# One more seven-product pair in the second MLP, and norm weights multiplied on VectorE: a hybrid decoder trunk on one core

## The chip, the cores and the metric

The kernel runs on one core of a Trainium2 chip. The metric is the device time of one execution in microseconds (us). The kernel before took 1081.53 us (median of three runs, 1081.48 to 1082.1). One execution was taken with the hardware profiler; that one has its own time, given below beside its span.

## The reference

The reference is a two-layer decoder trunk over 512 tokens of width 1024. Layer 0 is a gated short convolution followed by an MLP; after it a shared key and value side is computed. Layer 1 is a sparse attention followed by a second MLP; a final RMS norm ends it. The change is in the second MLP and in the final norm:

```python
def rms_norm(x, g):
    y = xf * lax.rsqrt(jnp.mean(xf * xf, axis=-1, keepdims=True) + EPS)
    return (y * g.astype(jnp.float32)).astype(x.dtype)

def squared_relu_mlp(h, w1, w2):
    return jnp.square(jax.nn.relu(h @ w1)) @ w2      # 1024 -> 4096 -> 1024
...
    x = x + squared_relu_mlp(rms_norm(x, norm_mlp[layer]), mlp_w1[layer], mlp_w2[layer])
return rms_norm(x, final_norm)
```

Everything is float32 in and out. The kernel writes each float32 factor as the sum of a high and a low float16 part and uses three products: high by high, high by low, low by high.

## The kernel before

**Layout.** Activations are kept turned: channels on the 128 partitions, tokens along the free side. `X` is the residual stream, eight tiles of 128 channels by 512 tokens.

**The MLP in two halves.** The 4096 hidden channels are done in two halves of 2048. In each half `mlp_up` makes eight column pairs `p` (256 hidden channels each) and `mlp_down` adds their part to `X` in four column pairs `p` (256 output channels each). The hidden values go to `rh` and `rl` (high and low parts), in seven combinations per pair, for the products of `mlp_down`.

**Two ways for an up pair.** An ordinary pair (`pair`, lines 410 to 412) takes eight chunks of the input, two column tiles and three products: 48 matmuls of 512 columns. A pair of the table `UP_SEVEN` goes through `seven` (line 687): it treats the product as 2x2 blocks and needs seven block products in place of eight: 84 matmuls of 256 columns. For that, its weights must be loaded as blocks and three VectorE instructions per piece add blocks together (lines 156 and 158). And its result is not ready in a bank at the end: four partial results are copied out of PSUM by ScalarE (`keep`, line 698), and three VectorE additions (lines 713, 716, 720) put them together. `seven` uses three accumulators: A and C, two buffers of bank `a` or of bank `c`, taken in turn from pair to pair, and E in bank `b`. A's first product is kept before A's second product is added to it in the same bank, and so on, so TensorE may not write on until the copy is done. After the products `put_relu` squares (ScalarE, line 666), forms differences (VectorE, lines 162 and 164), and writes `rh` (ScalarE, line 669) and `rl` (VectorE, line 670).

**Weights.** SyncE loads pieces of weights in a fixed order. A piece of blocks has 2048 numbers per partition and is loaded by two transfers of 256 KB into one of three buffers `wst2`; an ordinary piece has 1024 numbers per partition and is loaded by one transfer of 512 KB into one of three buffers `wst`. `convert_piece` turns a piece into `whi` and `wlo`. For blocks: sums on VectorE (lines 156, 158), `whi` on ScalarE (line 219), `wlo` on VectorE (line 220), 1792 numbers per partition, into four buffers. For an ordinary piece: `whi` on ScalarE (line 239) and `wlo` on VectorE (line 240), 1024 numbers. All weights of `mlp_down` are blocks: per column pair four pieces, which the text counts through as down piece 0 to 15. The load into a `wst2` buffer waits until the `wlo` of the piece before in that buffer is done.

**Down.** `mlp_down` makes seven products for eight chunks `c`, 21 matmuls of 256 columns each (line 833). Column pairs 0 and 2 use the banks b, b, a, a, and pairs 1 and 3 the banks d, e, c, c. `combine` (lines 799 to 814) adds the finished products into `X` on VectorE.

**The final norm's lead.** In the last half, `mlp_down` calls `mid_b(p)` in each column pair 1 to 3 (in pairs 1 and 2 behind chunk 5, in pair 3 behind chunk 3). It turns the finished column pair `p - 1` back to tokens by rows: eight transposes on TensorE (line 1555) into the two buffers of bank `a` or of bank `c`, four per buffer. Each buffer then holds two tiles of 128 tokens by 256 channels. For each tile ScalarE sums the squares (`square`, line 1551), copies the tile to `xt` (line 1566), and GpSimd multiplies the copy by the norm's weights (line 1567). The next column pair's products use the same two buffers again.

**The order.** The instructions are put in order by a scheduler when the program is built; each engine runs its own queue in that order, and waits on semaphores that the builder sets where two instructions touch the same buffer or the same PSUM bank.

Of the kernel before, what the change touches and what calls it, by code (L numbers as in the profile page):

```python
# [13 lines left out]
AF = mybir.ActivationFunctionType  # L14
OP = mybir.AluOpType
# [36 lines left out]
def body(ctx, tc, x, rel_bias, norm_mix, norm_mlp, mlp_w1, mlp_w2, a_w_in, a_conv_w, a_w_out,  # L52
# [3 lines left out]
    PE, ACT, DVE, POOL = nc.tensor, nc.scalar, nc.vector, nc.gpsimd  # L56
# [11 lines left out]
    def bank(tag, shape=(128, 512)):  # L68
        n = {"a": 2, "b": 2, "c": 2, "d": 1, "e": 1}[tag]
        return psum.tile(list(shape), F32, name=tag, bufs=n)  # L70
# [18 lines left out]
    def mlp_pieces(layer):  # L89

        for half in range(2):
            for p in range(8):
                (blocks if p in UP_SEVEN[layer][half] else block)(mlp_w1[layer], (8 * half + p) * 256, SW)
            for p in range(4):
# [10 lines left out]
            pieces.append(([v[c + k, :, :, c0:c0 + 256] for k in range(2)], None, scale))  # L105

    BY_SEVEN = ((2, 2), (3, 0), (3, 2))
    UP_SEVEN = (((4, 6), (0, 2, 4, 6)), ((6,), (0, 2, 4, 6)))

    v = a_w_in[0].rearrange("(c p) (s n) -> c p s n", p=128, s=3)  # L110
    for c in range(8):
# [315 lines left out]
    def ftile(name, bufs=2, n=S):  # L427
        return wk[0].tile([128, n], F32, name=name, bufs=bufs)
# [82 lines left out]
    for p in range(4):  # L511
# [57 lines left out]
        for i, dst in enumerate((pc, pu, pb)):  # L569
# [19 lines left out]
            for m in range(2):  # L589
                ch = 2 * p + m  # L590
                if dst is pc:
                    if m == 0:
                        tmps = []
                    t = ftile("cv_t", 2)
# [4 lines left out]
                elif dst is pu:  # L599
                    if m == 0:  # L600
                        convs = []
                    v = ftile("cv_v", 2, S + 2)
# [3 lines left out]
                    o = ftile("cv_o", 2)  # L606
# [38 lines left out]
    def mlp_up(xs, ss, rh, layer, half, rb, sums):  # L645
# [80 lines left out]
        def places():  # L726

            tags = 4 * ((wk[0], "up_s", 4),) + ((work, "ssacc", 1), (work, "sq", 1)) + 2 * ((work, "rb", 3),)
            for i in range(0, 8, 2):
                yield [u.tile([128, 4, 256], F16, name=name, bufs=n) for u, name, n in tags[i:i + 2]]  # L730
# [17 lines left out]
        at, staged_sums = places(), {}  # L748
        by_seven = UP_SEVEN[layer][half]
        early = half == 0 and layer == 0 and by_seven  # L750
# [779 lines left out]
    with pool("hidden_b") as hp:  # L1530
# [15 lines left out]
        def gains(p, n=2):  # L1546
            return fng[p // 2][:, (p % 2) * 256:(p % 2) * 256 + n * 128]

        def square(v, t, k, scale=1.0):
            junk = hp.tile([128, 8, 256], F32, name="ml_z", bufs=2)[:, 0, 0:v.shape[1]]  # L1550
            return ACT.activation(junk, v, AF.Square, scale=scale, accum_out=ssf[:, t, k:k + 1])

        def turn_tokens(ps, t, tiles):
            for m, ch in enumerate(tiles):
                PE.transpose(ps[:, m * 128:(m + 1) * 128], X[:, ch, t * 128:(t + 1) * 128], ident)

        def token_major(p, h, tag):

            ps = bank(tag)
            for i in range(2):  # L1560
                turn_tokens(ps[:, i * 256:(i + 1) * 256], 2 * h + i, (2 * p, 2 * p + 1))
            for i in range(2):
                t = 2 * h + i
                v, o = ps[:, i * 256:(i + 1) * 256], xt[t][:, p * 256:(p + 1) * 256]
                square(v, t, p)
                last = ACT.activation(o, v, AF.Copy)
                POOL.tensor_tensor(o, o, gains(p), op=OP.mult)
            return last

        def mid_b(p):  # L1570
            return [token_major(p - 1, h, "a" if p % 2 else "c") for h in range(2)][1]
# [126 lines left out]
```

## Time and profile before

| what | value |
|---|---|
| median of three runs | 1081.53 us |
| profiled execution: its time, its span | 1083.04 us, 1080.0 us |
| TensorE busy | 1067.5 us, 99% of the span |
| VectorE busy | 958.1 us, 89% |
| ScalarE busy | 621.7 us, 58% |
| GpSimd busy | 75.2 us, 7% |
| mean granted TensorE clock | 0.998 |

The second MLP's last half runs from 916.68 us (its first up pair) to the end. Its up pair 6 starts at 975.27, its ordinary pair 7 at 984.44, its down column pairs 0, 1, 2 and 3 at 994.80, 1013.14, 1032.35 and 1051.57, and the transposes of `mid_b` at 1026.90, 1046.11 and 1060.74.

In a row of a timeline stand the start, the duration, the engine and line, the operation and its tiles; the bracket behind it is the idle time just before and what ended it. In a row of the chain stand a start, a duration, the engine, the bank and line. In a row of the waits stand who waited for whom, the time in total, the number of waits and the longest.

### The profile page before, as it was taken

The numbers are of one execution on the slowest core, as the hardware profiler recorded it, in microseconds if no ns is written. First come the engines' busy times: TensorE is split into PE (matmuls) and PEld (weight loads), VectorE is DVE, ScalarE is ACT, GpSimd is POOL, SyncE is SP. The second block draws the span as 40 slices with busy tenths as digits, with TensorE's granted clock in tenths as the row PEclk, the third lists the DMA queues.
The fourth block names the chain that finished last, engine by engine and source line by source line (L and its number), as shares of the span: only waits on it lengthen the run. The fifth ranks groups of instructions, "written<-read, shape, count | busy, mean of one in ns | idle before, by whom it ended". The sixth has DMA issues, their size and how long they took to land.

```text
span 1080.0 us, 21256 instructions
## 1 busy us (share of the span) xinstructions
PE 1067.5 (99%) x8486; PEld 740.5 (69%) x8486; DVE 958.1 (89%) x1688; ACT 621.7 (58%) x974; POOL 75.2 (7%) x113
## 2 busy tenths in 40 slices
PE   9999999999999999999999999999999999999997
PEld 4446644477887758874867677775446788766896
DVE  5898757999998999999478899996999999999996
ACT  5663246565334674548577887874666433566453
POOL 1000000000000000000110104211000000002022
PEclk9999999999999999999999999999999999999999
DMA  8344124333433334312443442201542333333221
GB/s 260 112 147 134 40 81 154 125 99 109 137 101 115 104 113 155 119 44 95 126 139 102 143 138 81 61 21 60 166 127 70 106 111 124 98 101 98 98 99 78
DMA packets 117698, 118.50 MB, mean 110 GB/s; under 512 B 7276, under 2 KB 114496, under 8 KB 117600
## 3 DMA queue, kind: packets, MB, share of 16 engines
q1 hardware_dynamic: 114384, 110.77, 32.6%
q10 hardware_dynamic: 2512, 4.70, 1.3%
q0 software_dynamic: 704, 1.68, 0.5%
q8 instruction: 66, 1.08, 0.4%
q14 instruction: 32, 0.26, 0.1%
HBM read 110.22 MB, written 2.14 MB: 104 GB/s over the span
## 4 chain that ended last, share of the span: by engine, by line
PE 72%; DVE 18%; ACT 3%; issue 3%; DMA 3%; POOL 1%; SPq 0%; ACTq 0%; DVEq 0%; POOLq 0%
PE b L833 6%; PE c L411 5%; PE c L410 5%; PE c L412 4%; PE a L833 4%; PE c L833 4%; PE a L412 4%; PE a L687 4%; PE a L410 4%; PE a L411 4%; DVE wlo L220 4%; PE e L833 3%; PE b L412 3%; PE b L411 3%; PE c L1340 3%
## 5 line engine op out<-in xcount | busy, mean ns | idle before, releaser
L219 ACT ACTIVATE whi<-wst 128x1792 f16<-128x1792 f32 x92 | 153.9, 1692 | 120.9 <-DVE wst L158 72.1
L220 DVE SCALAR_TENSOR_TENSOR wlo<-wst,whi 128x1792 f16<-128x1792 f32 x92 | 185.5, 2022 | 6.5 <-ACT whi L219 6.4
L833 PEld LDWEIGHTS <-whi 128*128 128x128 f16 x1768 | 173.0, 98 | 20.3
L240 DVE SCALAR_TENSOR_TENSOR wlo<-wst,whi 128x1024 f16<-128x1024 f32 (+4 forms) x118 | 129.2, 1101 | 20.6 <-ACT whi L239 20.3
L239 ACT ACTIVATE whi<-wst 128x1024 f16<-128x1024 f32 (+4 forms) x118 | 111.1, 950 | 61.8 <-PE a L411 21.9
L412 PEld LDWEIGHTS <-wlo 128*128 128x128 f16 x800 | 78.1, 98 | 86.5 <-DVE wlo L240 1.0
L410 PEld LDWEIGHTS <-whi 128*128 128x128 f16 x800 | 78.2, 98 | 78.9 <-ACT whi L239 0.6
L411 PEld LDWEIGHTS <-whi 128*128 128x128 f16 x800 | 78.2, 98 | 78.4
L833 PEld LDWEIGHTS <-wlo 128*128 128x128 f16 x884 | 86.5, 98 | 10.9 <-DVE wlo L220 0.2
L669 ACT ACTIVATE rh<-ml_z 128x1792 f16<-128x1792 f32 x32 | 54.1, 1693 | 58.2 <-DVE ml_z L164 58.2
L411 PE MATMUL c<-xsl,whi 128*128 128x512 f16 x224 | 85.0, 379 | 0.0
L412 PE MATMUL c<-xsh,wlo 128*128 128x512 f16 x224 | 85.0, 379 | 0.0
L410 PE MATMUL c<-xsh,whi 128*128 128x512 f16 x224 | 85.0, 379 | 0.0
L1327 ACT ACTIVATE at_p<-at_s,at_m 128x384 f32<-128x384 f32 (+3 forms) x128 | 71.0, 556 | 20.9 <-DVE at_m L1325 20.7
L158 DVE TENSOR_TENSOR wst<-wst 128x256 f32<-128x256 f32 x184 | 78.3, 432 | 2.1
L156 DVE TENSOR_TENSOR wst<-wst 128x512 f32<-128x512 f32 x92 | 63.8, 697 | 15.3 <-DMA wst<-mlp_w_dram 15.1
L833 PE MATMUL b<-rh,whi 128*128 128x256 f16 x256 | 69.2, 273 | 0.0
L833 PE MATMUL b<-rh,wlo 128*128 128x256 f16 x256 | 69.2, 273 | 0.0
L833 PE MATMUL b<-rl,whi 128*128 128x256 f16 x256 | 67.8, 273 | 0.0
L687 PEld LDWEIGHTS <-whi 128*128 128x128 f16 x616 | 60.2, 98 | 7.9
L670 DVE TENSOR_TENSOR rl<-ml_z,rh 128x1792 f16<-128x1792 f32 x32 | 64.7, 2023 | 0.4 <-ACT rh L669 0.4
L1325 DVE CUSTOM_DVE_ANT_0 at_s<-b,T 128x384 f32<-128x384 f32 (+3 forms) x128 | 59.1, 485 | 4.9 <-PE b L1318 4.7
(437 smaller groups left out, 2911.7 us busy)
## 6 DMA issues: line engine op xcount, KB each, us to landing
wst<-mlp_w_dram SPq DMA_DIRECT2D x172, 256.0 KB, 2.9
wst<-mlp_w_dram SPq DMA_DIRECT2D x42, 512.0 KB, 3.7
wst<-a_w_in_dram SPq DMA_DIRECT2D x12, 512.0 KB, 3.5
wst<-w_kv_dram SPq DMA_DIRECT2D x12, 512.0 KB, 3.5
wst<-a_w_out_dram SPq DMA_DIRECT2D x8, 512.0 KB, 3.4
wst<-b_w_qg_dram SPq DMA_DIRECT2D x8, 512.0 KB, 3.6
wst<-b_w_o_dram SPq DMA_DIRECT2D x8, 512.0 KB, 3.6
T<-ext_d ACTq DMA_DIRECT2D x6, 528.0 KB, 3.9
```

The source lines that it names most:

```text
L158: DVE.tensor_tensor(b[:, :, o], b[:, :, x], b[:, :, y], op=OP.add)
L219: ACT.activation(hi, b[:, :, 1:], AF.Copy, scale=sc)
L220: lows[0] = DVE.scalar_tensor_tensor(lo, b[:, :, 1:], sc, hi, op0=OP.mult, op1=OP.subtract)
L239: ACT.activation(hi[:, s:e], w, AF.Copy, scale=sc)
L240: DVE.scalar_tensor_tensor(lo[:, s:e], w, sc, hi[:, s:e], op0=OP.mult, op1=OP.subtract)
L410: PE.matmul(ps, w[0], xs[0], start=start, stop=False, **k)
L411: PE.matmul(ps, w[0], xs[1], start=False, stop=False, **k)
L412: return PE.matmul(ps, w[1], xs[0], start=False, stop=stop, **k)
L670: DVE.tensor_tensor(rh[1][:, p], z[:, 1:8], rh[0][:, p], op=OP.subtract)
L687: PE.matmul(ps[:, 0:256], l, r, start=first and c == 0 and n == 0, stop=c == 3 and n == 2, skip_group_check=not first)
L833: mm = PE.matmul(acc7[i], wl if n == 1 else wh, xl if n == 2 else xh, stop=c == closes[i] and n == 2, start=c == 0 and n == 0 and not othe ...
L1327: self.weighed = ACT.activation(self.p[:, w], lg[:, w], AF.Exp, bias=mn[:, j:j + 1], scale=-1.0, accum_out=l[:, br * 4 + h:br * 4 + h + 1])
```

## The change

Two edits. The first puts pair 7 of the second MLP's second half into the table, so that it goes through `seven`; its two ordinary pieces of weights become two pieces of blocks. In that case the four kept results go to `dn_p`, `dn_w` and a new small tile `up_k`, since pair 7's own place in `rh` and `rl` is not free for them. The second edit is in `token_major`: for the first two column pairs VectorE multiplies the turned tile by the norm's weights straight from PSUM; ScalarE's copy and GpSimd's multiplication stay only for the third. Both edits are in the diff in full:

```diff
-    UP_SEVEN = (((4, 6), (0, 2, 4, 6)), ((6,), (0, 2, 4, 6)))
+    UP_SEVEN = (((4, 6), (0, 2, 4, 6)), ((6,), (0, 2, 4, 6, 7)))
...
             for i in range(2):
                 t = 2 * h + i
                 v, o = ps[:, i * 256:(i + 1) * 256], xt[t][:, p * 256:(p + 1) * 256]
-                square(v, t, p)
-                last = ACT.activation(o, v, AF.Copy)
-                POOL.tensor_tensor(o, o, gains(p), op=OP.mult)
+                last = square(v, t, p)
+                if p < 2:
+                    DVE.tensor_tensor(o, v, gains(p), op=OP.mult)
+                else:
+                    last = ACT.activation(o, v, AF.Copy)
+                    POOL.tensor_tensor(o, o, gains(p), op=OP.mult)
             return last
```

The new `DVE.tensor_tensor` is line 1567 of the changed kernel, and the old copy and multiplication are lines 1569 and 1570 there.

**ScalarE, up pairs 6 and 7.** `rl<-a` and `rh` are pair 6's last copy and pair 5's result; L219 rows are weights, whose numbers count up in the order of the pieces. Before:

```order
L698 ACTIVATE rl<-a 128x256
L219 ACTIVATE whi_12179<-wst_11936 128x1792
L669 ACTIVATE rh<-ml_z 128x1792
L219 ACTIVATE whi_12236<-wst_11992 128x1792
L219 ACTIVATE whi_12270<-wst_12049 128x1792
L1542 ACTIVATE up_s<-ident 128x128
L666 ACTIVATE ml_z<-ml_z 128x1024
L669 ACTIVATE rh<-ml_z 128x1792
```

Now:

```order
L698 ACTIVATE rl<-a 128x256
L669 ACTIVATE rh<-ml_z 128x1792
L219 ACTIVATE whi_12145<-wst_12045 128x1792
L698 ACTIVATE dn_p<-c 128x256
L698 ACTIVATE up_k<-c 128x256
L698 ACTIVATE dn_w<-c 128x256
L666 ACTIVATE ml_z<-ml_z 128x1024
L219 ACTIVATE whi_12232<-wst_12079 128x1792
L698 ACTIVATE dn_w<-c 128x256
```

The four copies of pair 7 are new. The first stands behind pair 5's L669 and the weights `whi_12145` (down piece 0), the last behind `whi_12232` (down piece 1).

**ScalarE, the turned tiles of the first column pair (`mid_b(1)`), with what each row waits for.** Before, the four squares and four copies stood together, and the next weights behind them. Now:

```order
L1551 ACTIVATE ml_z,ssf<-a 128x256 [waits PE_49]
L1551 ACTIVATE ml_z,ssf<-a 128x256 [waits DVE_49]
L1551 ACTIVATE ml_z,ssf<-a 128x256 [waits PE_49,Activation_49]
L1551 ACTIVATE ml_z,ssf<-a 128x256 [waits DVE_49]
L219 ACTIVATE whi_12753<-wst_12541 128x1792 [waits DMAHW7_49,DMAHW0_49]
```

The second and the fourth square now wait for VectorE: for the multiplication of the tile that shares their PSUM buffer.

**VectorE, the turned tiles of the second column pair (`mid_b(2)`).** Before, there were none of its rows here:

```order
L158 TENSOR_TENSOR wst_12797<-wst_12797 128x2x128 x2
L220 SCALAR_TENSOR_TENSOR wlo_12953<-wst_12736,whi_12952 128x1792
L220 SCALAR_TENSOR_TENSOR wlo_12981<-wst_12797,whi_12980 128x1792
L156 TENSOR_TENSOR wst_12853<-wst_12853 128x2x2x128
L799 SCALAR_TENSOR_TENSOR X<-b,X 128x256
```

Now:

```order
L158 TENSOR_TENSOR wst_12849<-wst_12849 128x2x128 x2
L220 SCALAR_TENSOR_TENSOR wlo_13001<-wst_12788,whi_13000 128x1792
L220 SCALAR_TENSOR_TENSOR wlo_13029<-wst_12849,whi_13028 128x1792
L1567 TENSOR_TENSOR xsh<-c,rb 128x256
L156 TENSOR_TENSOR wst_12905<-wst_12905 128x2x2x128
L1567 TENSOR_TENSOR xsh<-c,rb 128x256
L1567 TENSOR_TENSOR xsl<-c,rb 128x256
L799 SCALAR_TENSOR_TENSOR dn_w<-b,dn_p 128x256
L158 TENSOR_TENSOR wst_12905<-wst_12905 128x2x128
L1567 TENSOR_TENSOR xsl<-c,rb 128x256
```

The four multiplications stand behind the `wlo` of down pieces 13 and 14, with the sums of piece 15 between them. Column pair 3's products in bank `c` wait, in the built program, for the second and the fourth of them, where they waited for ScalarE's copies before.

## The prediction

> **What bounds the kernel now.** I read the page's busy line and chain first, then the waits of TensorE, then the windows of the stretch that the change touches.
>
> ```profile
> PE 1067.5 (99%) x8486; PEld 740.5 (69%) x8486; DVE 958.1 (89%) x1688; ACT 621.7 (58%) x974; POOL 75.2 (7%) x113
> PE 72%; DVE 18%; ACT 3%; issue 3%; DMA 3%; POOL 1%; SPq 0%; ACTq 0%; DVEq 0%; POOLq 0%
> ```
> ```profile
> PE c L1340 <- DVE at_pl L1346: 2.3, 6, 0.8
> ```
>
> TensorE is busy for 99% of the span, and its largest group of waits is 2.3 us. A microsecond of products saved is a microsecond of the kernel, as long as the operands and the banks come in time. The windows (length, then busy time of PE, PEld, DVE, ACT, POOL) show how much room the others have:
>
> ```profile
> 975.30:994.80 19.50, 19.50 (x134) 12.89 (x133) 19.06 (x24) 13.07 (x14) 5.26 (x3) 1.00 0.26 82
> 994.80:1013.10 18.30, 18.30 (x171) 16.39 (x169) 18.20 (x24) 9.41 (x7) 1.91 (x1) 1.00 0.30 99
> 1013.10:1032.40 19.30, 19.30 (x179) 17.41 (x177) 17.51 (x29) 9.98 (x18) 3.42 (x4) 1.00 0.29 98
> 1032.40:1051.60 19.20, 19.20 (x178) 17.30 (x176) 18.07 (x25) 9.40 (x15) 1.05 (x1) 1.00 0.34 111
> ```
>
> TensorE never stops there, but VectorE has only 0.44, 0.1, 1.8 and 1.1 us free in four stretches. That is the bound behind the bound: what is added on VectorE stays as lateness until one of those gaps takes it.
>
> **What the change saves on TensorE.** The chain gives both prices:
>
> ```profile
> 975.27 3.93 PE a L687 x36
> 980.51 3.93 PE a L687 x36
> 994.80 1.31 PE b L833 x12
> ```
>
> Pair 6, by seven products, takes 975.27 to 984.44 (980.51 + 3.93): 9.17 us. Pair 7, ordinary, takes 984.44 to 994.80: 10.36. So at most 1.19 us are saved, and one product of seven (12 matmuls) is 1.31.
>
> **What it adds on VectorE.** The prices, start to start where one instruction follows another:
>
> ```profile
> 972.73 0.69 DVE L156 TENSOR_TENSOR wst<-wst 128x512 f32<-128x512 f32 x1
> 973.33 0.43 DVE L164 TENSOR_TENSOR ml_z<-ml_z 128x256 f32<-128x256 f32 x1
> 974.00 0.43 DVE L164 TENSOR_TENSOR ml_z<-ml_z 128x256 f32<-128x256 f32 x1
> 978.28 1.28 DVE L664 SCALAR_TENSOR_TENSOR ml_z<-c,rb 128x512 f32<-128x512 f32 x2
> 979.81 1.22 DVE L240 SCALAR_TENSOR_TENSOR wlo<-wst,whi 128x1024 f16<-128x1024 f32 x1
> 981.88 0.42 DVE L713 TENSOR_TENSOR ml_z<-b,rh 128x256 f32<-128x256 f32 x1
> 985.02 2.03 DVE L220 SCALAR_TENSOR_TENSOR wlo<-wst,whi 128x1792 f16<-128x1792 f32 x1
> ```
>
> An L156 costs 0.60 (972.73 to 973.33), a 256-wide addition 0.33 (two between 973.33 and 974.00), a wide `wlo` 1.93 (0.1 of its 2.03 overlaps its successor). Pair 7's two block pieces cost 2 x (0.60 + 2 x 0.33 + 1.93) = 6.4. Lines 713, 716 and 720 add 3 x 0.33 = 1.0, its own L661s some 1.3. Two L240 (2 x 1.13) and L664 (1.2) go. Net: +5.2 us in the stretch with 0.44 us free. ScalarE gets four copies of 0.28 and 1.3 for the wider `whi`s, about 2.4, where it had 6 us free. The eight multiplications cost VectorE 8 x 0.33 = 2.7 us; the nearest row is L713 above, 128x256 out of PSUM at 0.42 end to end. Bounds for one: 0.27 (ScalarE's copies, below) to 0.43.
>
> I then followed both queues row by row in the changed order with these prices, each row starting when the row before it has issued and its operands are ready. The prices below are all from rows; the times are estimates.
>
> **Place 1, pairs 6 and 7.**
>
> ```profile
> 974.52 1.70 ACT L669 ACTIVATE rh<-ml_z 128x1792 f16<-128x1792 f32 x1 [3.14 <-DVE ml_z L164]
> 976.62 0.38 ACT L698 ACTIVATE rh<-a 128x256 f32<-128x256 f32 x1 [0.40 <-PE a L687]
> 984.20 1.70 ACT L669 ACTIVATE rh<-ml_z 128x1792 f16<-128x1792 f32 x1 [0.37 <-DVE ml_z L164]
> 985.80 3.27 ACT L219 ACTIVATE whi<-wst 128x1792 f16<-128x1792 f32 x2
> ```
>
> Pair 7's first `wlo` now stands on VectorE ahead of pair 4's L164s: they end at 976.02 instead of 974.43, so L669 starts at 976.1, and pair 6's first copy, which needed only 976.62, ends at 978.1. TensorE wants that bank two products into the pair, at 975.27 + 2.62 = 977.89: 0.25 lost. Pair 7 starts at 984.7; its first product ends near 986.0, but its first copy stands behind pair 5's L669 (984.7 to 986.3) and a `whi` of 1.6 (two take 3.27): it ends at 988.3, where TensorE wants the bank at 984.7 + 2.62 = 987.3. That loses 1.05. The fourth copy stands behind the next `whi`, which waits for sums on VectorE that end at 992.35; it ends at 994.4, 0.8 late. The last product ends near 995.75, so down starts there instead of at 994.80: **+0.95**, not -1.19. The saving is eaten by waits of 2.1.
>
> **Place 2, down's first two column pairs.** VectorE runs some 4 us late here: down piece 0's `wlo`, at 985.02 above, now starts near 988.7. The thinnest margin I find is piece 3's, ready at 1009.1 and used at 1009.5: nothing, if the prices hold; lost in the bad case, 0.5.
>
> **Place 3, turning column pair 0.** Down starts 0.95 late, so the transposes, too.
>
> ```profile
> 1026.90 0.87 PE a L1555 x8
> 1032.35 1.31 PE b L833 x12
> 950.56 2.03 DVE L220 SCALAR_TENSOR_TENSOR wlo<-wst,whi 128x1792 f16<-128x1792 f32 x1
> 956.10 0.69 DVE L156 TENSOR_TENSOR wst<-wst 128x512 f32<-128x512 f32 x1 [0.97 <-DMA wst<-mlp_w_dram]
> 1029.86 3.34 ACT L219 ACTIVATE whi<-wst 128x1792 f16<-128x1792 f32 x2
> ```
>
> The rows between down piece 0's `wlo` and the first multiplication are 42.9 us of VectorE's queue by the prices, so that multiplication comes at 1031.6, 2.8 after its square. The second square must wait for it. Then VectorE stands at an L156 whose load waits for a buffer: from a `wlo`'s end to the sums that use its buffer again took 952.6 to 956.1, so 3.5 us, and here it leads to 1033.2. The other multiplications end at 1034.2, 1034.5 and 1035.6, and ScalarE's next `whi`, queued behind the fourth square, starts at 1035.0 instead of 1029.86. Column pair 2 starts at 1033.35 and waits 0.5 for the second buffer of bank a, 0.3 for that weight's `wlo`, and 0.2 at the next transposes: **+1.0**.
>
> [...] Were reads free to overlap, the second square would start some 3 us earlier, and about 0.5 of this term would go.
>
> **Place 4, turning column pair 1.** This is the largest term.
>
> ```profile
> 1046.11 0.87 PE c L1555 x8
> 1051.57 0.66 PE d L833 x6
> 1052.88 0.98 PE c L833 x9
> 1044.03 2.02 DVE L220 SCALAR_TENSOR_TENSOR wlo<-wst,whi 128x1792 f16<-128x1792 f32 x1
> 1048.28 3.96 DVE L220 SCALAR_TENSOR_TENSOR wlo<-wst,whi 128x1792 f16<-128x1792 f32 x2 [1.10 <-ACT whi L219]
> 1046.55 3.29 ACT L219 ACTIVATE whi<-wst 128x1792 f16<-128x1792 f32 x2 [2.86 <-PE c L1555]
> 1051.96 0.43 ACT L1566 ACTIVATE xsl<-c 128x256 f32<-128x256 f32 x1
> ```
>
> Before, bank c was read out by ScalarE's last copy at 1052.39, and TensorE wanted it at 1052.88: 0.5 us of margin. Now the four multiplications stand behind the two `wlo` of 1048.28, which wait for the two `whi` of 1046.55, which wait for sums on a late VectorE: `wlo` of piece 12 goes from 1044.03 to 1048.95, the `whi`s from 1046.55 to 1051.35, the `wlo`s from 1048.28 to 1053.1. They end at 1056.96; the first multiplication starts there, the second ends at 1058.4, the fourth at 1059.7. Column pair 3 starts at 1053.5 (+1.95) and wants bank c 1.3 later, at 1054.8: a stall of 3.6 for the first buffer, then 0.7 for the second: **+4.3**. Behind it nothing more is late: the last weight's `wlo` is done at 1064.4, before its first use, and the third column pair is turned as before.
>
> **Sum.** +0.95 + 1.0 + 4.3 = +6.25. The profiled execution (1083.04) would become 1089.3; it lies 1.5 above the median, so the median becomes 1081.53 + 6.25 = **1087.8**. Bounds of prices: all VectorE prices as end-to-end instead of start-to-start (0.1 more on perhaps 15 instructions between two gaps) push place 4 out by 1.5; a VectorE that recovers 1.5 us more in its gaps takes as much off. Own range 1086.2 to 1089.2.
>
> **Rivals.**
>
> *VectorE catches up in part.*
>
> ```profile
> 1029.35 0.81 DVE L156 TENSOR_TENSOR wst<-wst 128x512 f32<-128x512 f32 x1 [1.39 <-DMA wst<-mlp_w_dram]
> 1030.19 1.72 DVE L158 TENSOR_TENSOR wst<-wst 128x256 f32<-128x256 f32 x2
> ```
>
> While GpSimd multiplied the first tiles before, these rows took 1.0 us more than their like (0.69, and two L158s in 0.8). That goes away, but my prices are the undisturbed ones and hold this gain already. For more, pieces would have to load sooner than after 3.5 us, or the gaps be larger than the 0.1 and 1.8 us in 37.6. With 2 to 3 us recovered over the two stages, place 4 is 1 to 2.5 and place 3 is 0.2: +2.2 to +5, some 1085.
>
> *Half clock after the stall.*
>
> ```profile
> 1073.00:1074.00 1.00, 0.12 (x3) 0.00 (x0) 0.90 (x6) 0.83 (x4) 0.11 (x1) 1.00 0.71 291
> 1076.00:1077.00 1.00, 0.00 (x0) 0.00 (x0) 0.12 (x1) 0.03 (x1) 0.00 (x0) 0.70 0.99 397
> 1077.00:1078.00 1.00, 0.00 (x0) 0.00 (x0) 0.00 (x0) 0.00 (x0) 0.00 (x0) 0.50 0.94 375
> ```
>
> The last matmul ends near 1073.1, the clock is still 1.00 and is 0.70 in the slice from 1076, so it falls about 3.3 us after the last work. A stall of 3.6 lies just beyond. Half clock for the some 3.5 us that the trace shows to its end costs half of that: +1.7, so 1089.5. Against: the stall is an estimate with 1 us either way, and the fall may not start at once. [...]
>
> *Only place 1 and small waits.* If the two `wlo`s of place 4 aren't late (margin enough after VectorE's gaps), the sum is +1 to +2.2: 1082.5 to 1083.7, no difference that a measurement can tell (under 0.2%, 2.2 us).
>
> *Faster: pair 7's saving arrives.* If pair 7's copies don't wait (ScalarE takes L669 before 984.7 because VectorE is not late), and bank c is read in time, what is left is the 1.19 saved: 1080.3. It decides at the first copy of pair 7: it must end by 987.3. Against it is that the copy stands two long rows (3.2 us) behind a sum of VectorE's, which has 0.44 us free; and 1.19 is under what a measurement can tell, unless the relief from GpSimd shown above shortens a wait of TensorE by another us.
>
> **Chances.** Main 0.55, partial catch-up 0.17, half clock 0.08: slower, 0.80. Small waits 0.10: the same. The faster side 0.10, of which I give 0.07 to more than 0.2% and 0.03 to less: faster 0.07, the same 0.13. The range 1083.6 to 1090.0 reaches from the lower end of the partial catch-up (1081.53 + 2.2 = 1083.7) to the half clock with half a microsecond to spare, and leaves out the two cases below it, 0.2.
>
> **What would show it.** Place 1: pair 7's copies (L698 out of bank c) right behind L669 and L219, a wait of TensorE on them of 1 us, down starting near 995.8. Place 3: squares in bank a waiting for L1567. Place 4: a wait of TensorE's L833 in bank c on L1567 of 3 to 4 us, the two `wlo` ahead of it ending near 1057. The prediction is wrong if down starts before 994.8, or if the first multiplication in bank c starts before 1055.

## The result, and the profile after

The changed kernel took 1090.1 us (median of six executions) against 1081.69 us before, or +8.4 us. One of the six, the profiled one, ran throughout at a TensorE clock of 0.65 and took 1594.29 us; the other five took 1089.62 to 1090.77 us (median 1089.81), and the ratio, 1.0077 with a 95% interval of 1.0063 to 1.0090, is worked out from them. I had forecast +6.25 (1087.8) and a range up to 1090.0; the kernel became slower, as forecast, and the median of the six lies 0.1 us above that range. The profile shown is that of a repeat: 1090.67 us, ratio 1.0082 (1.0067 to 1.0097); its profiled execution took 1091.26 us with a span of 1089.4.

The page of the repeat, and the waits of TensorE in it (who waited for whom, total, times, longest):

```profile
PE 1070.9 (98%) x8522; PEld 745.5 (68%) x8522; DVE 963.0 (88%) x1706; ACT 622.1 (57%) x970; POOL 61.3 (6%) x105
```
```profile
PE c L833 <- DVE xsh L1567: 3.5, 1, 3.5
PE c L1340 <- DVE at_pl L1346: 2.4, 6, 0.8
PE c L289 <- DVE any L921: 1.3, 1, 1.3
PE c L687 <- ACT dn_p L698: 0.9, 1, 0.9
PE c L687 <- ACT dn_w L698: 0.6, 1, 0.6
PE a L833 <- DVE xsl L1567: 0.6, 1, 0.6
PE a L687 <- ACT rh L698: 0.5, 1, 0.5
PE a L833 <- DVE xsh L1567: 0.4, 1, 0.4
```

The second and third rows are older than the change. The others are new, and they are the waits that the prediction named: pair 7's copies (L698 to `dn_p`, `dn_w`), pair 6's first copy, bank a behind the first multiplications, and bank c behind the second column pair's. TensorE is busy for 3.4 us more than before (1070.9 against 1067.5) although its products became shorter; where that comes from shows in the granted clock. Windows of the repeat around the wait at bank c (length, busy time of PE, PEld, DVE, ACT, POOL, then PEclk):

```profile
1054.00:1056.00 2.00, 1.56 (x15) 1.15 (x12) 2.00 (x2) 1.91 (x4) 0.00 (x0) 1.00 0.13 46
1056.00:1058.00 2.00, 0.00 (x0) 0.00 (x0) 2.00 (x3) 0.00 (x0) 0.00 (x0) 1.00 0.01 4
1058.00:1060.00 2.00, 0.96 (x5) 0.72 (x6) 2.00 (x7) 1.31 (x6) 0.00 (x0) 0.53 0.00 0
1060.00:1062.00 2.00, 2.00 (x11) 1.19 (x10) 2.00 (x8) 0.92 (x1) 0.00 (x0) 0.50 0.00 0
1062.00:1064.00 2.00, 2.00 (x12) 1.39 (x10) 1.97 (x4) 0.78 (x1) 0.00 (x0) 0.50 0.00 0
1064.00:1066.00 2.00, 2.00 (x16) 1.64 (x15) 1.97 (x4) 0.00 (x0) 0.00 (x0) 0.77 0.00 0
```

TensorE stands from 1055.6 to 1059.0. The clock halves at 1058.1 and is back at 1064.9, so for some 6 us the products after the wait run at half speed: 11 or 12 matmuls in 2 us, where the same count gives 21 from 1066 on, at a clock of 1.00.

To see where the time went I take the start of each stage from TensorE's timeline: pair 6, down, and the three groups of transposes. These are the two executions' lengths of stage; the last stage runs from the third transposes to the last token tiles' products (first L843 into bank b).

| stage | before, us | repeat, us | difference | forecast |
|---|---|---|---|---|
| pairs 6 and 7 | 975.11 to 994.64: 19.53 | 974.65 to 995.48: 20.83 | +1.30 | +0.95 |
| down to the first transposes | 32.09 | 32.10 | 0 | 0 |
| first to second transposes | 19.22 | 20.84 | +1.62 | +1.0 |
| second to third transposes | 14.62 | 21.39 | +6.77 | +4.3 |
| from there | 9.21 | 9.02 | -0.2 | 0 |

In the fourth row the waits are 4.1 us (0.2 at the transposes, 3.64 and 0.22 at bank c) and the other 2.7 are the clock. A wait given to a hundredth, like 3.64, is the time lost between two products' starts; the rows of the waits count from the end of the product before and show 0.16 less (3.47). The stages add up to +9.5, like the two profiled spans (1089.4 against 1080.0), and the medians only to +8.4 and +8.9. Of the nine executions of the changed kernel that the two ratios use, the profiled one has the lowest mean clock (0.995; the others 0.996 or 0.997), so part of its 6.8 us at half clock may be its own; that is not shown. The start at 974.65 instead of 975.11 is a difference of work long before the change.

### The profile page after: what moved, and what is told of

Its sections match the earlier page's. It is cut to its first block, busy times and chain, and to the rows that moved or that the text cites. A ratio compares the mean times of both kernels' runs of the same rounds, so it can differ in the third digit from the quotient of the medians.

```text
span 1592.5 us, 21338 instructions
## 1 busy us (share of the span) xinstructions
PE 1584.0 (99%) x8522; PEld 927.1 (58%) x8522; DVE 986.4 (62%) x1706; ACT 631.9 (40%) x970; POOL 61.8 (4%) x105
## 4 chain that ended last, share of the span: by engine, by line
PE 99%; DVE 0%; issue 0%; ACT 0%; DVEq 0%; ACTq 0%
PE a L687 8%; PE b L833 8%; PE c L412 6%; PE c L410 6%; PE c L411 6%; PE a L833 6%; PE c L833 6%; PE a L411 5%; PE a L412 5%; PE a L410 5%; PE e L833 4%; PE d L833 4%; PE b L410 4%; PE b L412 4%; PE b L411 4%; PE c L1340 3%
## 5 line engine op out<-in xcount | busy, mean ns | idle before, releaser
L833 PEld LDWEIGHTS <-whi 128*128 128x128 f16 x1768 | 211.9, 120 | 77.0 <-issue 0.6
L220 DVE SCALAR_TENSOR_TENSOR wlo<-wst,whi 128x1792 f16<-128x1792 f32 x94 | 189.9, 2021 | 73.7 <-ACT whi L219 73.4
L219 ACT ACTIVATE whi<-wst 128x1792 f16<-128x1792 f32 x94 | 158.2, 1692 | 168.5 <-PE a L833 65.8
L412 PEld LDWEIGHTS <-wlo 128*128 128x128 f16 x784 | 95.1, 121 | 145.0 <-issue 142.0
L411 PEld LDWEIGHTS <-whi 128*128 128x128 f16 x784 | 93.8, 120 | 134.9 <-issue 130.5
L410 PEld LDWEIGHTS <-whi 128*128 128x128 f16 x784 | 94.6, 121 | 132.8 <-issue 127.4
L833 PEld LDWEIGHTS <-wlo 128*128 128x128 f16 x884 | 106.1, 120 | 38.8 <-DVE ml_z L664 0.6
L412 PE MATMUL c<-xsh,wlo 128*128 128x512 f16 x208 | 106.9, 514 | 0.0
L410 PE MATMUL c<-xsh,whi 128*128 128x512 f16 x208 | 106.8, 514 | 0.0
L411 PE MATMUL c<-xsl,whi 128*128 128x512 f16 x208 | 106.7, 513 | 0.0
L687 PEld LDWEIGHTS <-whi 128*128 128x128 f16 x672 | 80.5, 120 | 30.7 <-issue 1.9
L833 PE MATMUL b<-rh,wlo 128*128 128x256 f16 x256 | 89.1, 350 | 0.0
L833 PE MATMUL b<-rh,whi 128*128 128x256 f16 x256 | 88.9, 349 | 0.0
L833 PE MATMUL b<-rl,whi 128*128 128x256 f16 x256 | 87.1, 349 | 0.0
L158 DVE TENSOR_TENSOR wst<-wst 128x256 f32<-128x256 f32 x188 | 77.5, 419 | 2.0
L1343 ACT ACTIVATE at_ph<-c 128x512 f16<-128x512 f32 (+1 forms) x88 | 48.7, 553 | 61.0 <-PE c L1340 58.5
L669 ACT ACTIVATE rh<-ml_z 128x1792 f16<-128x1792 f32 x32 | 54.0, 1691 | 47.0 <-DVE ml_z L164 47.0
L156 DVE TENSOR_TENSOR wst<-wst 128x512 f32<-128x512 f32 x94 | 64.1, 684 | 10.0 <-DMA wst<-mlp_w_dram 10.0
```

What stands on the lines that cost most here:

```text
L156: DVE.tensor_tensor(b[:, :, 4:7:2], b[:, :, 0:1].to_broadcast(two), b[:, :, 2:0:-1], op=OP.add)
L158: DVE.tensor_tensor(b[:, :, o], b[:, :, x], b[:, :, y], op=OP.add)
L219: ACT.activation(hi, b[:, :, 1:], AF.Copy, scale=sc)
L220: lows[0] = DVE.scalar_tensor_tensor(lo, b[:, :, 1:], sc, hi, op0=OP.mult, op1=OP.subtract)
L410: PE.matmul(ps, w[0], xs[0], start=start, stop=False, **k)
L411: PE.matmul(ps, w[0], xs[1], start=False, stop=False, **k)
```

## The experiments

All differences are to the kernel before, run on the same chip beside each. "Pairs", "first to second" and "second to third" mean the stages of the table above; the forecasts on record say "around column pair 2" and "at bank c of column pair 3" for the waits in the last two.

**The change once more.** No edit.

> The change once more, for an undisturbed trace of it. Theory 1 (late VectorE, no more): TensorE waits of 2.1 us in pairs 6 and 7, 1.0 us around column pair 2, 4.3 us at bank c of column pair 3, sum +6.25, and the clock stays at 1.00 until the last products; the measured +8.4 then needs about 2 us more of waits at places I did not name. Theory 2 (half clock as well): the same waits, and behind the wait at bank c of column pair 3 some 3 to 4 us in which the granted clock is 0.50, worth 1.7 to 2 us: +8.0 to +8.4. Theory 3 (the waits at bank c are not 3.6 but 5 us or more because VectorE is later than I worked out): +8, clock 1.00.

Measured: +8.9 us (1090.67; 1089.87 to 1091.73). This is Theory 2: the waits stand where they were worked out, the stages add up to 7.0 us without the clock's part against 6.25, and the clock falls. Theory 3 is ruled out, since the longest wait is 3.5.

**Each edit alone.**

```diff
# pair 7 alone
-                if p < 2:
+                if p < 0:
# the multiplication alone
-    ... ((6,), (0, 2, 4, 6, 7)))
+    ... ((6,), (0, 2, 4, 6)))
```

> The first edit alone (pair 7 by seven products; ScalarE's copies and GpSimd's multiplications as before). Theory 1, by the same prices along its queues: +0.95 at the pairs, nothing around column pair 2, 0.8 us at bank c of column pair 3 because ScalarE's copies come behind two late conversions: +1.7, 1083.3 us. Theory 2: no wait over 2 us, so no half clock: also +1.7. Rival (VectorE catches up by then): +1.0, 1082.6 us. Rival (pair 7's lateness is the main cost): over 1085 us.

> The second edit alone (pair 7 ordinary; VectorE multiplies out of PSUM for two column pairs). Theory 1: VectorE is in time at the pairs, but the four multiplications in bank c still stand behind two weight conversions: a wait of 3.6 us for the first buffer, 0.7 for the second, sum +4.4, 1086.0 us. Theory 2: with that wait of 3.6 us the clock falls here, too: another 1.7 to 2, some 1088 us. Rival (the waits at bank c come from pair 7's lateness): under 1082.6 us.

Measured, pair 7 alone: 1085.43, ratio 1.0032 (1.0019 to 1.0044), +3.6 us. By stage: +1.04 at the pairs, 0, 0, +2.06, +0.55. The wait at bank c on ScalarE's copies was 1.04 and 0.63 rather than 0.8 in all, and one that I had not worked out stands at the third transposes. The total is 1.9 us above Theory 1, and over the 1085 us of the rival that has pair 7's lateness as the main cost: 1.0 of the 3.6 us stand at the pairs, 2.6 behind them. Its waits:

```profile
PE c L687 <- ACT dn_p L698: 0.9, 1, 0.9
PE c L833 <- ACT xsh L1569: 0.9, 1, 0.9
PE c L687 <- ACT dn_w L698: 0.6, 1, 0.6
PE c L833 <- ACT xsl L1569: 0.5, 1, 0.5
PE a L1555 <- DVE X L814: 0.5, 1, 0.5
```

Measured, the multiplication alone: 1087.09 (1086.37 to 1089.19), ratio 1.0052 (1.0037 to 1.0067), +5.3 us, between Theory 1 and Theory 2. The pairs are untouched (19.53), and the wait at bank c is there in full, 3.8 us, with the clock down from 1056.4 to 1059.8. So the rival that it comes from pair 7's lateness is ruled out as the only source. The mechanism can be read off this kernel's ScalarE (first rows) and VectorE (second rows), since here nothing of pair 7 is mixed in:

```profile
1026.16 0.38 ACT L1551 ACTIVATE ml_z<-a 128x256 f32<-128x256 f32 x1 [3.52 <-PE a L1555]
1030.40 0.39 ACT L1551 ACTIVATE ml_z<-a 128x256 f32<-128x256 f32 x1 [3.77 <-DVE xsh L1567]
...
1031.73 0.39 ACT L1551 ACTIVATE ml_z<-a 128x256 f32<-128x256 f32 x1 [0.49 <-DVE xsl L1567]
...
1032.11 3.27 ACT L219 ACTIVATE whi<-wst 128x1792 f16<-128x1792 f32 x2
```
```profile
1028.42 0.69 DVE L156 TENSOR_TENSOR wst<-wst 128x512 f32<-128x512 f32 x1 [1.44 <-DMA wst<-mlp_w_dram]
1029.15 0.89 DVE L158 TENSOR_TENSOR wst<-wst 128x256 f32<-128x256 f32 x2
1029.95 0.41 DVE L1567 TENSOR_TENSOR xsh<-a,rb 128x256 f32<-128x256 f32 x1
...
1050.57 3.96 DVE L220 SCALAR_TENSOR_TENSOR wlo<-wst,whi 128x1792 f16<-128x1792 f32 x2 [1.37 <-ACT whi L219]
1054.44 0.41 DVE L1567 TENSOR_TENSOR xsh<-c,rb 128x256 f32<-128x256 f32 x1
```

This execution was 1.2 us ahead of the one of before at that point (transposes at 1025.52, 1026.73 there). ScalarE's first square is done at 1026.6. Its multiplication stands on VectorE behind sums whose load comes late, and starts at 1029.95. The second square waits for it (3.77 us in its row), and it holds up the whole queue: the two conversions that began at 1029.86 before now begin at 1032.11, though they have nothing to do with the norm. One column pair later VectorE is still late by more than 2 us (its two `wlo` at 1050.57 instead of 1048.28), and the multiplications out of bank c stand behind them.

**The multiplication for one column pair only**, with pair 7 by seven.

```diff
-                if p < 2:
+                if p < 1:        # the first column pair
+                if p == 1:       # in another kernel, the second
```

> Pair 7 by seven products, and VectorE's multiplication for the first column pair alone; the second column pair goes by ScalarE's copies and GpSimd as before. Theory 1: +0.95 at the pairs, 1.0 around column pair 2, 1.8 at bank c of column pair 3 (two waits of 1.2 and 0.6): +3.7, 1085.3 us. Theory 2: no wait over 3 us, so no half clock and the same +3.7; the gap to the whole change is then 4 to 5 us, of which only 2.5 us are waits. Theory 3 (VectorE later than worked out): over +5.

> Pair 7 by seven, and VectorE's multiplication for the second column pair alone. No turns are taken around column pair 2, so ScalarE's weights are not held there. Queue sum: +1.3 at the pairs, 2.6 and 0.7 at bank c: +4.6 without a fall of the clock, 1086.2. If a fall needs a window of some 3.4 us that is mostly without work, a wait of 2.6 brings it in none or some executions: between 1086 and 1088 us, spread by 1.7. If the clock followed any wait over 2 us, 1088 in all of them.

Measured, the first column pair only: 1086.72, +4.9 us (ratio 1.0046, 1.0031 to 1.0061): +1.5 at the pairs, +1.46 and +2.05 behind, +0.4 at the end, clock at 1.00. Each term was a little larger than in the sum. Measured, the second only: 1088.29, +7.0 us (1.0061, 1.0046 to 1.0076): a wait of 3.36 at bank c and 0.4 behind it, at half clock, instead of 2.6 and 0.7, and the clock down from 1056.9 to 1060.3 in the profiled execution; the mean clock was 0.995 or 0.996 in all four. Without any turns taken around column pair 2, pair 7's lateness alone brings the same wait about. Either source is enough.

**Work for TensorE in the wait.**

```diff
+                            if mid and p == 3 and c + k == 0 and i == 4:
+                                for _ in range(32):
+                                    PE.matmul(acc7[0], zeros[0], rh[0][:, 0, 0], start=False, stop=False, ...)
```

> The whole change, with 32 matmuls of 256 columns added on TensorE ahead of the first product that waits for bank c in column pair 3. They multiply zeros into an accumulator that is open, so nothing in the result changes; they take 3.5 us, about as long as TensorE stood still there. Theory (half clock): the granted clock stays at 1.00 to the last products, and the 2.7 us that the products after the wait took longer come back: 1087.4 us. Rival (the products after the wait were slow for operands, not for the clock): no gain, 1090 us or more.

`zeros` is a tile of zeros that GpSimd fills once. Measured: 1088.54 (1088.03 to 1088.66; ratio 1.0062, 1.0045 to 1.0079), +7.2 us. The change itself was +8.9 in the repeat and +8.4 in the first measurement, so the kernel is 1.2 to 1.7 us faster for doing 32 matmuls more. The raw times are 2.1 apart, but they come from two chips, and the two intervals overlap; the forecast of 1087.4 was not reached. The profile is clearer than the times. Windows of this kernel over the same place:

```profile
1056.00:1057.00 1.00, 1.00 (x11) 0.90 (x10) 1.00 (x1) 0.00 (x0) 0.00 (x0) 1.00 0.03 8
1060.00:1061.00 1.00, 0.94 (x9) 0.85 (x10) 1.00 (x5) 0.25 (x1) 0.00 (x0) 1.00 0.00 0
1062.00:1063.00 1.00, 1.00 (x11) 0.90 (x10) 0.97 (x2) 0.44 (x1) 0.00 (x0) 1.00 0.00 0
```

The clock stays at 1.00 and the stage from the second to the third transposes takes 19.19 us instead of 21.39. The bank comes no earlier (first product there at 1058.69). So 2.2 us of that stage were the clock. That is 0.5 less than the 2.7 above, because at full clock the next buffer of bank c is waited for longer (0.69 instead of 0.22). The rival, slow operands, is ruled out.

**Both squares of a buffer ahead of its two multiplications.**

```diff
-            for i in range(2):
-                ...
-                last = square(v, t, p)
+            sq = [square(v2[i], 2 * h + i, p) for i in range(2)] if p < 2 else None
+            for i in range(2):
+                last = sq[i] if p < 2 else square(v, t, p)
```

> The second edit alone, with both squares of a PSUM buffer issued before its two multiplications, so that ScalarE hands each buffer over once and waits for no multiplication. Theory A (taking turns is the cost: ScalarE's weights queue behind a square that waits for VectorE): ScalarE's conversions come 2 us earlier, the multiplications of the second column pair start near when bank c is wanted, a wait of about 0.5 us instead of 3.9: 1082.2 us. Theory B (the multiplications' place behind two weight conversions is the cost): the wait stays over 3 us, 1085 us or more.

> Both edits, with both squares of a buffer ahead of its two multiplications. Theory A: the pairs cost +1.3 as in the change; no waits around column pair 2; about 2 us at bank c, where pair 7's lateness on VectorE still shows; too short for the clock to fall: 1085 us. Theory B: 1088 us or more. Rival (without the turns pair 7's lateness is covered): 1082.9 us, only the 1.3 at the pairs.

Measured, without pair 7: 1082.58, ratio 1.0010 (1.0001 to 1.0019), +1.3 us in place of +5.3. This fits Theory A, though the wait left at bank c is 1.0 and not 0.5. In its ScalarE rows the four squares run through and the conversions follow at once:

```profile
1026.95 0.38 ACT L1551 ACTIVATE ml_z<-a 128x256 f32<-128x256 f32 x1 [3.62 <-PE a L1555]
...
1028.04 0.39 ACT L1551 ACTIVATE ml_z<-a 128x256 f32<-128x256 f32 x1
1028.30 0.22 ACT L1551 ACTIVATION_READ_ACCUMULATOR ml_z<-a 128x1 f32 x1
1028.39 3.30 ACT L219 ACTIVATE whi<-wst 128x1792 f16<-128x1792 f32 x2
```

Measured, with pair 7: 1087.92, ratio 1.0058 (1.0043 to 1.0073), +6.6 us, where I had expected 1085. The wait around column pair 2 is gone (19.21 between the transposes), but the one at bank c is 3.55 instead of 2, and the clock falls. So taking turns is not the whole cause: with pair 7's lateness the multiplications come as late as with the turns:

```profile
1047.49 0.69 DVE L156 TENSOR_TENSOR wst<-wst 128x512 f32<-128x512 f32 x1 [0.46 <-DMA wst<-mlp_w_dram]
...
1052.34 3.96 DVE L220 SCALAR_TENSOR_TENSOR wlo<-wst,whi 128x1792 f16<-128x1792 f32 x2 [1.09 <-ACT whi L219]
1056.22 0.74 DVE L1567 TENSOR_TENSOR xsh<-c,rb 128x256 f32<-128x256 f32 x2
```

**The conversion of down piece 0 behind pair 7's first copy**, with pair 7 alone.

```diff
-            cv = ahead()
+            AHEAD2[0], cv = (2 if layer and half and p == 6 else 3), ahead()
```

> Pair 7 by seven, norm as before (like the run of the first edit alone, +3.6), with down piece 0's conversion kept back until pair 7's first copy. Theory (VectorE is full, and what is late only shows where a wait ends last): the waits of 1.1 and 0.8 on pair 7's copies go, the saving of 1.2 arrives at the pairs, and a wait of about 1.4 on a weight's low part appears in down's first column pairs; in all +3 to +3.6, no real gain. Rival (the copies' place behind ScalarE's conversion is the cost by itself): +1.7, the 1.9 us come back.

`AHEAD2` is how many pieces of blocks may be converted ahead of their use; it is 3 elsewhere in this MLP. Measured: 1085.88, +4.4 us (1.0041, 1.0026 to 1.0056). Pair 7's copies come in time, pairs 6 and 7 take 18.84 us (0.7 less than before), and in the next stage TensorE stands for a weight's low part, as forecast:

```profile
PE b L833 <- DVE wlo L220: 1.5, 1, 1.5
```

The saving of the first edit arrived and was paid out again 14 us later. Against the kernel before, the total is worse by 0.7 us than the first edit alone, a little more than the theory had; the two intervals overlap, so that it is no better is what the run shows.

**VectorE relieved of 3.9 us.** In the kernel with both edits and both squares ahead, pair 7's two low parts are left out, and its high parts are multiplied in their place.

```diff
-            lows[0] = DVE.scalar_tensor_tensor(lo, ...)
-            ready[i] = (hi, lo)
+            if i < len(pieces) - 18 or i > len(pieces) - 17: lows[0] = DVE.scalar_tensor_tensor(lo, ...)
+            ready[i] = (hi, hi if len(pieces) - i in (17, 18) else lo)
```

> Both edits with both squares ahead of the multiplications, and the two low parts of pair 7's weights left out (their high parts are used twice, so the result is another): 3.9 us less on VectorE ahead of the pairs. Theory (the lateness is VectorE's load from pair 7): the waits on pair 7's copies go and pair 6 and 7 take 18.5 to 18.8 us (19.5 before, 20.8 in the change); at bank c a wait of 2 to 3 us stays, since VectorE has no gap in which the rest of pair 7's work and the multiplications fit; +1 to +3. Rival (pair 7's copies wait for TensorE's or ScalarE's own order, whatever VectorE does): the pairs stay at 20.6 us or more.

Measured: 1085.91, +4.4 us (1.0038, 1.0023 to 1.0053), against +6.6 with the low parts. Pairs 6 and 7 take 18.48 us: with less on VectorE, 1.05 of the 1.19 us arrive. Behind them 1.2 us are waited at bank a and 2.3 at bank c, and the clock falls again; that fall I had not put into the expectation of +1 to +3. One of its four executions took 1084.44 us at a mean clock of 0.998, the others 1085.66 to 1086.17 at 0.996 and 0.997: perhaps one without the fall, but no trace of it was kept.

**GpSimd's multiplications left out** for the first two column pairs (those channels stay without the norm's weights), with pair 7 alone.

```diff
-                    POOL.tensor_tensor(o, o, gains(p), op=OP.mult)
+                    if p == 2: POOL.tensor_tensor(o, o, gains(p), op=OP.mult)
```

> Pair 7 by seven and ScalarE's copies, with GpSimd's multiplications by the norm's weights left out for the first two column pairs (so these are not multiplied at all). In the run of the first edit alone TensorE waited 1.1 us at the third column pair's transposes for VectorE's last additions into X, while GpSimd multiplied. Theory (GpSimd's multiplications slow VectorE's sums beside them): that wait goes and the wait at bank c shrinks from 1.7 to about 0.8; +3.6 becomes +1.7. Rival (VectorE's lateness alone makes it): +3.6 stays.

Measured: 1084.33, +2.8 us (1.0026, 1.0016 to 1.0037). The wait at the third transposes goes (the last two stages take +1.67 and -0.2 instead of +2.06 and +0.55), the one at bank c stays 1.04 and 0.63: that is 0.8 of the 1.9 us that the theory asked for. VectorE's sums beside and without GpSimd, first in the kernel of pair 7 alone, then in this one:

```profile
1055.37 1.22 DVE L156 TENSOR_TENSOR wst<-wst 128x512 f32<-128x512 f32 x1
1056.51 0.41 DVE L799 SCALAR_TENSOR_TENSOR X<-b,X 128x256 f32<-128x256 f32 x1
1057.17 0.97 DVE L158 TENSOR_TENSOR wst<-wst 128x256 f32<-128x256 f32 x1
```
```profile
1055.17 0.68 DVE L156 TENSOR_TENSOR wst<-wst 128x512 f32<-128x512 f32 x1
1056.44 0.42 DVE L158 TENSOR_TENSOR wst<-wst 128x256 f32<-128x256 f32 x1
```

GpSimd multiplies from 1053.76 to 1058.73 in the first kernel, and not at all in these rows of the second. The rows show which sums are slowed: this L156 takes 0.54 and this L158 0.55 longer beside GpSimd's multiplications, while L799 stays at 0.41 and the two `wlo` just ahead, the second of them beside GpSimd, at 3.96 in both kernels. Why these and not the others, the rows do not show.

**The squares ahead of the conversions.** The whole change, with the second column pair's squares put where the first's stand.

```diff
-                        behind = squared if p == 1 else None
+                        behind = squared if p < 3 else None
```

> The whole change, with the four squares of the second column pair ahead of the two weight conversions on ScalarE. Theory (VectorE has no room; a wait moved is not a wait saved): bank c comes in time, but the conversions and with them the additions into X are late, and TensorE waits some 3.7 us at the third transposes instead: +8 to +8.5 with the clock's fall, no gain. Rival (the place behind two conversions is all there is to it): the 3.9 us at bank c and the clock's fall go, 1084.5 us.

Measured: 1089.80, +8.3 us (1.0078, 1.0062 to 1.0095). Bank c comes in time, and the same length of wait stands elsewhere:

```profile
PE a L1555 <- DVE X L812: 3.7, 1, 3.7
```

This fits the theory: VectorE has no room, and a wait moved is not a wait saved. The rival (1084.5) is ruled out.

No version here beats the kernel before. The nearest is the multiplication alone with both squares ahead, 1.3 us slower.

## Why the prediction was right or wrong

**Direction and waits: right.** That VectorE was the bound behind the bound, that pair 7's saving would be eaten at its own copies, and that bank c would be the largest term, all show in the profile after at the places named. ScalarE at the pairs, in the repeat:

```profile
984.53 1.70 ACT L669 ACTIVATE rh<-ml_z 128x1792 f16<-128x1792 f32 x1 [2.13 <-DVE ml_z L164]
986.14 1.68 ACT L219 ACTIVATE whi<-wst 128x1792 f16<-128x1792 f32 x1
987.73 0.36 ACT L698 ACTIVATE dn_p<-c 128x256 f32<-128x256 f32 x1
...
993.75 0.37 ACT L698 ACTIVATE dn_w<-c 128x256 f32<-128x256 f32 x1
```

I had the first copy ending at 988.3 and the last at 994.4; they end at 988.1 and 994.1. The waits of TensorE between products were 0.63, 1.07 and 0.79 where I had 0.25, 1.05 and 0.8. Removing 3.9 us from VectorE (the kernel without pair 7's low parts) brought the saving, and so did another place in ScalarE's queue (down piece 0 behind the first copy). So both halves of the cause of place 1 are shown: VectorE is late, and the copies stand behind what waits for it.

**The step that failed: the clock stood among the rivals with 0.08, not in the sum.** The sum was 6.25 and it came out at 7.0 in the table (1.30 + 1.62 + 4.1), and at +7.2 in the kernel that kept its clock; what lifts the total to +8.4 is half clock, 1.2 to 1.7 us by the medians and 2.2 in the profiled executions' stage. I weighed it by the one fall in the trace of before, 3.3 us after the last matmul, and took this for a stall that TensorE must exceed. It isn't. Five profiles show their clock behind the last matmul: it falls 3.3 us after it (before), 3.2 (the repeat), 4.2 (pair 7 alone), 2.3 (the multiplication alone) and 3.8 (the first column pair only), so the 3.3 was one value of a spread. These are the one of before and all the falls ahead of the end, with TensorE's stop, its next product, and the clock's fall and return:

| kernel | stop | next product | fall | return | low for |
|---|---|---|---|---|---|
| before (its end) | 1073.1 | none | 1076.4 | none seen | |
| repeat of the change | 1055.6 | 1059.0 | 1058.1 | 1064.9 | 6.8 |
| multiplication alone | 1052.1 | 1055.9 | 1056.4 | 1059.8 | 3.4 |
| second column pair only | 1053.3 | 1056.5 | 1056.9 | 1060.3 | 3.4 |
| both, squares ahead | 1053.6 | 1057.0 | 1057.3 | 1060.7 | 3.4 |
| without pair 7's low parts | 1052.9 | 1055.2 | 1056.1 | 1059.5 | 3.4 |
| squares ahead of the conversions | 1062.6 | 1066.3 | 1067.8 | 1071.2 | 3.4 |

The fall comes 2.5 to 5.2 us after the stop, in five of the six kernels once products run again, and it lasts 3.4 us or twice that. Every wait of 2.3 us or more was followed by one; no wait of 1.5 or less was. The falls also lie whole numbers of such lengths apart, where the clock shows it up to the end: in the repeat the clock falls again 27.3 us after the first fall (0.80 on average over 1080 to 1089 puts that fall at 1085.4), in the multiplication alone 23.9 (0.53 over 1080 to 1085, so 1080.3), which is 8 and 7 times 3.41. A stall need not fill such a length: in the 3.4 us before the last fall of the table TensorE stood for 1.9 us only. So the stall of 3.6 was long enough, and the 0.08 too low. The limits that the expectations name for a fall (a wait over 2 us, one over 3 us, some 3.4 us mostly without work) were guesses of mine; the runs showed the 2.3 and the 1.5 above.

**Terms mis-sized.** Place 1 was put at 0.95 and measured 1.3, by the wait on pair 6's first copy. Place 3 was put at 1.0 and measured 1.6: the waits at bank a were 0.52 and 0.79, where I had one of 0.5, on the second buffer, with 0.3 for a low part and 0.2 at the transposes. Place 4's wait was put at 4.3 and measured 3.9. That its first part came out as worked out (3.64 for 3.6) is in part luck: TensorE wanted the bank at 1055.4 and got it at 1059.0, both 0.6 later than worked out. VectorE in the repeat, where I had the two `wlo` from 1053.1 and the first multiplication at 1056.96:

```profile
1053.72 3.96 DVE L220 SCALAR_TENSOR_TENSOR wlo<-wst,whi 128x1792 f16<-128x1792 f32 x2 [1.09 <-ACT whi L219]
1057.60 0.41 DVE L1567 TENSOR_TENSOR xsh<-c,rb 128x256 f32<-128x256 f32 x1
```

**Two sums that do not come out.** Of the partial catch-up I wrote +2.2 to +5; its own terms (0.95, 0.2 and 1 to 2.5) give +2.2 to +3.7. My own range should read 1086.3 to 1089.3.

**The cause of place 4 was half right.** I derived it from one lateness, carried from pair 7 on, with the turns of place 3 as a small term. The runs show two sources, each enough alone: the turns (multiplication alone, 3.8) and pair 7's lateness (both edits with squares ahead, 3.4). Without both it is 0.9. My remark that "about 0.5 of this term" would go if reads need not take turns priced only the wait on the spot, and not the conversions queued behind the waiting square; the rows show the square's wait (3.34 us on the first multiplication in the repeat), but no run shows whether the two reads could overlap. That the wait would just go with the squares ahead of the conversions, the rival of the last run, was wrong too: it came back at the transposes.

**The rivals.** The partial catch-up did not occur: VectorE is no less late than worked out (rows above). The case of small waits is ruled out by the same two `wlo`, and the faster one by pair 7's first copy, which came at 988.1 and not by 987.3. GpSimd's relief was rightly left out of the gain, since the changed kernel's prices were undisturbed ones; but it made the forecast for pair 7 alone too low by 0.8 of the 1.9 us.

## What to carry to other kernels

An engine that is 95% busy over 76 us (VectorE in the four windows of the prediction) has hardly a free place: work put there came out as a wait at the next spot where that engine ended last, and in two of three runs another order only moved the spot. The third order, both squares ahead, did save 4 us (+1.3 in place of +5.3, without pair 7), because it took away a wait of one queue for another. Where two engines read one PSUM buffer, hand it over once: a reader that waits for the other's turn also holds up the unrelated work queued behind it (here weight conversions, 2.2 us). And a wait of TensorE of the length of those in the table, 2.3 us and more, is to be counted with what follows it: an estimate of up to 1.7 us, half of 3.4, for each 3.4 us at half clock.

## What was not expected of the hardware

The clock's fall is the main one: it follows waits as short as 2.3 us, comes up to 5.2 us after the stop, and costs up to 1.7 us per 3.4 us, an estimate from the clock of 0.50. Products of zeros into an open accumulator kept the clock at 1.00, and the kernel with more matmuls was the faster one, by 1.2 to 1.7 us. How much idle time precedes a fall can be bounded by counting it over 3.41 us at a time. In the 3.41 us that end with a fall, the six kernels of the table have 2.5, 2.9, 3.1, 3.1, 2.3 and 1.9 us, in its order. In the six changed kernels without a fall ahead of the end, no 3.41 us from 970 us to the last matmul held more than 1.5 (the first column pair only). The closest pair comes from one kernel (the last row): counted back from its fall at 1067.8, its wait from 1062.6 to 1066.3 is split at 1064.4, and the clock stayed at 1.00 after the first part, 1.8 us, and fell after the second, 1.9, a difference no larger than the tenths given here. If falls keep to such steps, a wait of 2.3 us could be split so that neither part reaches 1.8; that is an estimate from these numbers, and no run shows such a wait. What stays open is the border for the return: the clock came back after 3.4 us with 0.3 us idle (the multiplication alone), and stayed low after 3.4 us with 0.9 (the repeat).
